# Three changes of order around the expert loop of a two-block transformer kernel: where the next stage's weight casts stand, where the router's transposes stand, and which engine sums the router's squares

## The chip, the cores and the metric

The kernel runs on one core of a Trainium2 chip, in one launch. The metric is the device time of that launch in microseconds (us); less is better. Times are medians over several runs, and one execution of each kernel is recorded by the hardware profiler.

## The reference

256 tokens of width 1024 in float32 pass through two transformer blocks. The stages at which the change works are the first block's mixture of experts and the feed-forward layer that follows it:

```python
def hierarchical_moe(h, ...):          # h = rmsnorm(x, norm_ffn_g)
    t = h.reshape(-1, D)
    p_group = softmax(t @ w_route_group + b_route_group)          # 4 groups, the best one is taken
    e_logits = t @ w_route_expert[g] + b_route_expert             # 8 experts in it, the best two are taken
    ...
    gates = ...                                                   # [32 experts, tokens]
    for wg, wu, wd, ge in experts:                                # 32 experts, width 512
        y = y + ge[:, None] * ((silu(t @ wg) * (t @ wu)) @ wd)
    return y
...
x = x + memory_cross_attention(...)                               # ends in @ w_mo
x = x + hierarchical_moe(rmsnorm(x, norm_ffn_g), ...)
x = rmsnorm(x, final_g)                                           # end of block 1
x = x + 0.5 * swiglu(rmsnorm(x, ffn1_norm), w13, w2)              # block 2 begins: the "first ffn"
```

Block 2 goes on with a linear recurrence, a second feed-forward layer, a shared key and value projection, a third feed-forward layer, stick-breaking attention of 16 heads and a fourth feed-forward layer.

## The kernel before, in words

The activations lie channels first, `xT` [128, 8 chunks, 256 tokens]. A normal product is three matmuls (lines 177 to 179): weights and activations are each split into a rounded part and a rest (`wh`, `wl` and `xgh`, `xgl`), and the product of the two rests is left out. `wload` (line 139) loads 1 MB of weights into a buffer `raw` by SyncE's queue (line 149), casts it to `wh` in two halves on ScalarE (ACT, line 157) and subtracts on VectorE (DVE, line 158).

The experts work in plain float32 on weights as loaded. 16 buffers form a ring for loads of 1 MB: 8 `raw`, 6 that `wh` and `wl` otherwise use, 2 that `xgh` and `xgl` otherwise use (`wraw`, line 161; DMA on line 171). An expert needs four loads `w_gu` and two `w_down`. A token takes a slot of 64 per expert.

- **Router** (`route`, line 696). Each block of two chunks of `xT` is finished on DVE (`update`, line 334) out of the last product's accumulators `acc0` to `acc3`. Its squares (ACT, line 272) are summed over channels by TensorE (PE) with one-column matmuls (line 275), 32 in all; `rstd` (line 291) and a chain of small DVE operations make the reciprocal root, copied to `my` (line 793). The logits are a product with 36 columns, copied to `lt` (line 716). `tokens` (line 805) transposes the normed input to tokens-first with 32 matmuls (line 813) and eight ACT copies (line 814); then the logits are transposed (line 721), scaled (`lg`, line 724), and some 25 DVE operations choose the experts (`ow`, `w`); line 743 counts positions on PE, one-hot matrices follow (line 831), then the gather by matmul (line 846) and the first expert product (line 941).
- **Expert loop** (`experts`, line 818). Per expert: `w_gu` products (line 941), `gu` on ACT (line 886), transposes (line 951), `sl` and `hx` (lines 953, 955), and one expert later the `w_down` products (line 967), `yh` on ACT (line 971), `yl` on DVE (line 972) and the scatter back to tokens by `combine` (line 982) into `acc0` to `acc3`. Expert 30 is followed by a branch (lines 799, 800), not taken here, for tokens beyond the 64 slots; the engines pass it together with SyncE.
- **First ffn** (`after_moe`, line 1022, then `ffn`). `update` adds the experts' sum to `xT`; squares on ACT and one-column sums on PE (again lines 272 and 275), splits (lines 221, 222), products.

A scheduler orders the instructions of each engine by their readiness in its own model, except where `after` (line 128) adds an order without a wait, as `pe` (line 925) does for the loop's matmuls while `s.queue` is a list. Matmul results go to two PSUM tags A and B of two buffers each, which `ps()` takes by turns unless a tag is named.

Of the kernel before, what the change touches and what calls it, by code (L numbers as in the profile page):

```python
# [8 lines left out]
F32 = mybir.dt.float32  # L9
# [3 lines left out]
ALU = mybir.AluOpType  # L13
# [3 lines left out]
P = 128  # L17
T = 256
D = 1024
KC = D // P  # L20
# [27 lines left out]
class Block:  # L48
    def __init__(s, ctx, tc, io):
        s.tc, s.nc, s.ctx, s.io = tc, tc.nc, ctx, io  # L50
        s.n = s.turn = s.place = 0
        s.queue = None
        pool = lambda name, bufs, **k: ctx.enter_context(tc.tile_pool(name=name, bufs=bufs, **k))
        s.cp = pool("const", 1)
        s.wp = pool("weights", 3)
        s.tp = pool("temps", 2)
        s.xp = pool("x", 1)
        s.pa = pool("acc", 1, space=PSUM)
        s.pp = pool("ps", 2, space=PSUM)
# [76 lines left out]
    def wload(s, views, C, N, parts=1, between=None):  # L136

        nc = s.nc
        full = C * N == 2048
        raw = s.new(s.wp, [P, 2048], "raw", F32, RAW)  # L140
        wh = s.new(s.wp, [P, 2048], "wh", F32R, WHL)
        wl = s.new(s.wp, [P, 2048], "wl", F32R, WHL)
        v = lambda t: t[:, :C * N].rearrange("p (c n) -> p c n", n=N)
        if not isinstance(views, list):
            n = C // parts
            views = [views[:, i * n:(i + 1) * n] for i in range(parts)]
        c = 0
        for i, view in enumerate(views):
            nc.sync.dma_start(v(raw)[:, c:c + view.shape[1]], view)
            c += view.shape[1]  # L150
            if between is not None:
                between(i)
        cuts = max(parts, 2) if full else parts
        n = C * N // cuts
        for i in range(cuts):
            lo, hi = i * n, (i + 1) * n
            nc.scalar.copy(wh[:, lo:hi], raw[:, lo:hi])  # L157
            nc.vector.tensor_sub(wl[:, lo:hi], raw[:, lo:hi], wh[:, lo:hi].bitcast(F32))  # L158
        return v(wh), v(wl)

    def wraw(s, view, C, N, n=None):
# [81 lines left out]
            nc.vector.scalar_tensor_tensor(y, u, 1.5, y, op0=ALU.add, op1=ALU.mult)  # L243
        return y

    def sums(s):

        return {"n": 0, "st": s.new(s.tp, [P, T], "ssq")}

    def ssq(s, st, x):  # L250

# [10 lines left out]
    def sums_pe(s, w=None):  # L262

        n = 1 if w is None else w.shape[2]
        return {"n": 0, "w": w, "pe": s.ps([P, 2, n], "B")}

    def ssq_pe(s, st, x, q=None):
        k, out = st["n"], st["pe"]
# [8 lines left out]
    def colsum(s, st, out):  # L277

        for h in range(2):
            s.nc.tensor.matmul(out[:, h:h + 1], st["st"][:, h * P:(h + 1) * P], s.ones[:, 0:1], start=True, stop=True)  # L280
        return out

    def bank(s, tag="acc3"):
# [45 lines left out]
    def update(s, ps, b, scale, xg, g, st):  # L329

        nc = s.nc
        xs = s.xT[:, 2 * b:2 * b + 2]
        if scale == 1.0:
            nc.vector.tensor_add(xs, ps, xs)
        else:
            nc.vector.scalar_tensor_tensor(xs, ps, scale, xs, op0=ALU.mult, op1=ALU.add)
        if xg is None:
            return
        if st is not None and "pe" in st:
            for m in (2 * b, 2 * b + 1):  # L340
                s.ssq_pe(st, s.xT[:, m])
        for m in (2 * b, 2 * b + 1):
            s.split(xg, m, s.xT[:, m], g[:, m:m + 1])
            if st is not None and "pe" not in st:
                s.ssq(st, s.xT[:, m])

    def rowproj(s, w, K):
# [30 lines left out]
                done(acc[b], b)  # L378
        return step, tail

    def residual(s, scale, g, sums=None):

        xg, st = s.pair(s.xp, KC, "xg"), (sums or s.sums)()
        return xg, st, lambda ps, b: s.update(ps, b, scale, xg, g, st)


# [239 lines left out]
    def mem_attention(s, p1, xg, rows, km, vm):  # L626
        nc, io = s.nc, s.io
# [39 lines left out]
        p = scores(0, query(0))  # L667
        for h in range(1, 4):
            q = query(h)
            pT = turn(p)  # L670
            p = scores(h, q)
# [2 lines left out]
        pT = turn(p)  # L674
        step(1, hl(1))
        values(3, pT)
        xg, st, done = s.residual(1.0, s.col("norm_ffn_g", 0, 8), s.sums_pe)
        tail([(2, hl(2)), (3, hl(3))], done)
        return xg, st

# [14 lines left out]
    def route(s, xg, rows):  # L695


        nc, t = s.nc, s.mt
# [5 lines left out]
        raw = s.tmp([P, P])  # L704
# [9 lines left out]
        s.proj(ps, wr, 0, xg, m=36)  # L714
        lt = s.new(t, [36, T], "lt")
        nc.vector.tensor_copy(lt, ps)
        s.tokens(xg)
        y = rows()
        pl = s.ps([P, 2, 36])
        for h in range(2):  # L720
            nc.tensor.transpose(pl[:, h], lt[:, h * P:(h + 1) * P], s.ident[0:36, 0:36])
        lg = s.new(t, [P, 2, 36], "lg")
        for h in range(2):
            nc.vector.scalar_tensor_tensor(lg[:, h], pl[:, h], y[:, h:h + 1], s.col("b_route", 0, 36), op0=ALU.mult, op1=ALU.add)
# [60 lines left out]
    def moe(s, mt, xg, st):  # L785
        nc = s.nc
        s.mt = mt
        y = []

        def rows():  # L790
            y.append(s.rstd(st["pe"].rearrange("p h n -> p (h n)"), D)[1])
            y.append(s.new(mt, [P, 2], "my"))
            nc.vector.tensor_copy(y[1], y[0])
            return y[0]
        pos, gs, gates, over, fi = s.route(xg, rows)
        with s.tc.tile_pool(name="experts", bufs=1) as me:
            def rest():

                flag = nc.values_load(fi[0:1, 0:1], min_val=0, max_val=1)
                with s.tc.If(flag > 0):  # L800
                    s.moe_over(over, y[1])
            acc = s.experts(me, pos, gs, gates, rest)
        return acc

    def tokens(s, xg):

        s.tok = s.pair(s.mt, 2, "tok", N=D)
        for k in range(0, KC, 2):
            for src, dst in zip(xg, s.tok):
                pt = s.ps([P, 2, 2, P])  # L810
                for j in range(2):
                    for h in range(2):
                        s.nc.tensor.matmul(pt[:, h, j], src[:, k + j, h * P:(h + 1) * P], s.idr, start=True, stop=True)
                s.nc.scalar.copy(dst[:, :, k * P:(k + 2) * P], pt.rearrange("p h j b -> p h (j b)"))

    def experts(s, mt, pos, gs, gates, rest):
# [141 lines left out]
    def expert_down(s, mt, e, hx, oT, gt):  # L958


        nc = s.nc
        pd = s.ps([P, 512], "A")
        for t in range(2):
            def use(w):
                for c in range(2):
                    for n in range(2):
                        s.pe(nc.tensor.matmul(pd[n * CAP:(n + 1) * CAP], hx[:, 2 * t + c], w[:, c, n * 512:n * 512 + 512],  # L967
                                              start=t + c == 0, stop=t + c == 2))
            s.expert_weights(use)
        yh, yl = (s.new(mt, [P, 512], n, F32R) for n in ("yh", "yl"))  # L970
        nc.scalar.mul(yh, pd, gt[:, 0:1])
        nc.vector.scalar_tensor_tensor(yl, pd, gt[:, 0:1], yh.bitcast(F32), op0=ALU.mult, op1=ALU.subtract)
        return yh, yl

    def combine(s, acc, e, y, oT):
# [325 lines left out]
    def run(s):  # L1301
# [8 lines left out]
        with tc.tile_pool(name="second", bufs=1) as p2:  # L1310
# [3 lines left out]
            ffn = lambda xg, rows, n, l, g, *more: s.ffn(  # L1314
                p2, xg, rows, io[f"ffn{n}_w13_2"][l], io[f"ffn{n}_w2_2"][l], g, *more)
            xg, rows = ffn(xg, rows, 1, 0, gains("mix_norm_2", 0), None, rescale)
            with tc.tile_pool(name="rglru", bufs=1) as pr:
                xg, rows = s.rglru(pr, xg, rows, gains("ffn2_norm_2", 0))
            with tc.tile_pool(name="attn", bufs=1) as pk:
# [82 lines left out]
```

## Time and profile before

| what | value |
|---|---|
| median of 3 runs | 1717.57 us (1716.57 to 1721.44) |
| the profiled execution's own time | 1718.19 us |
| its span in the profile | 1716.4 us, mean granted TensorE clock 0.984 |
| busy in the span | PE 97%, DVE 54%, ACT 41% |
| moved by DMA | 408 MB, 238 GB/s over the span |

The stages in the profiled span: mixer and memory attention to about 239 us, router to about 257, expert loop to about 705, last expert to about 731, first ffn from there on. PE's busy time is modelled in the profile, and the granted clock says at which share of its full speed TensorE ran. "Idle before" is an engine's waiting time ahead of an instruction, with what ended it.

### The profile page before, as it was taken

To read this page: it belongs to the slowest core of one execution; us is meant where nothing else is said; L and a number is where in the kernel's file an instruction comes from. 1 tells how busy PE (TensorE), PEld (TensorE's weight loads), DVE (VectorE), ACT (ScalarE), POOL (GpSimd) and SP (SyncE) were. 2 spreads that over 40 slices of the span, in tenths; PEclk is the share of its full clock that TensorE was granted. 3 is DMA by queue.
4 is the path that set the end of the run, shared out by engine and by line. 5 is a ranking of instruction groups with operands and counts; after the bars stand their busy time and mean duration, and the time that the engine had idled before them with its cause. 6 is when DMAs were issued, how large, how long until landed. Compare 5 with 4: busy or idle time off the path is not lost.

```text
span 1716.4 us, 28131 instructions
## 1 busy us (share of the span) xinstructions
PE 1659.7 (97%) x11883; PEld 1349.5 (79%) x11883; DVE 922.9 (54%) x1618; ACT 704.0 (41%) x1138; POOL 5.0 (0%) x19
## 2 busy tenths in 40 slices
PE   8999989999999998699999999999999999999998
PEld 7878984444444443299999999999899997689998
DVE  7998741111111110265657886556755558876554
ACT  8526532111111111244445754445644446764442
POOL 0000000000000000000000000000000000000000
PEclk9999989999999999889999999999999999899999
DMA  9334359999999999845553555554555454044530
GB/s 367 132 120 175 142 226 367 419 419 420 419 419 419 420 419 420 361 183 191 197 184 136 197 221 172 197 184 161 198 196 197 174 195 172 25 148 172 197 123 26
DMA packets 60227, 408.03 MB, mean 238 GB/s; under 512 B 6592, under 2 KB 9920, under 8 KB 11456
## 3 DMA queue, kind: packets, MB, share of 16 engines
q1 hardware_dynamic: 60096, 406.18, 61.4%
q8 instruction: 95, 1.56, 0.4%
q14 instruction: 36, 0.29, 0.0%
HBM read 405.11 MB, written 1.05 MB: 237 GB/s over the span
## 4 chain that ended last, share of the span: by engine, by line
PE 54%; DVE 2%; ACT 1%; issue 1%; DMA 0%; SPq 0%; ACTq 0%; DVEq 0%
PE A L179 6%; PE A L178 6%; PE A L177 6%; PE acc L177 5%; PE acc L178 5%; PE B L177 5%; PE B L178 5%; PE acc L179 5%; PE B L179 5%; ACT wh L157 1%; PE A L1262 1%; DVE wl L158 1%; PE A L967 1%; PE B L416 0%; PE B L408 0%
## 5 line engine op out<-in xcount | busy, mean ns | idle before, releaser
L157 ACT CAST wh<-raw 128x1024 fp32r<-128x1024 f32 (+2 forms) x378 | 378.0, 1034 | 445.0 <-issue 363.8
L158 DVE TENSOR_TENSOR wl<-raw,wh 128x1024 fp32r<-128x1024 f32 (+2 forms) x378 | 448.6, 1204 | 160.5 <-ACT wh L157 159.7
L177 PE MATMUL B<-xgh,wh 128*128 128x256 f32 x872 | 246.1, 282 | 6.9 <-ACT wh L157 6.9
L177 PE MATMUL A<-xgh,wh 128*128 128x256 f32 (+1 forms) x872 | 246.7, 283 | 0.0
L179 PE MATMUL A<-xgh,wl 128*128 128x256 f32 (+1 forms) x872 | 245.5, 282 | 0.1
L178 PE MATMUL A<-xgl,wh 128*128 128x256 f32 (+1 forms) x872 | 245.5, 282 | 0.1
L179 PE MATMUL B<-xgh,wl 128*128 128x256 f32 x872 | 245.6, 282 | 0.0
L178 PE MATMUL B<-xgl,wh 128*128 128x256 f32 x872 | 245.2, 281 | 0.0
L178 PE MATMUL acc<-hl,wh 128*128 128x256 f32 x704 | 194.7, 278 | 0.2
L179 PE MATMUL acc<-hh,wl 128*128 128x256 f32 x704 | 194.5, 277 | 0.0
L177 PE MATMUL acc<-hh,wh 128*128 128x256 f32 x704 | 193.1, 278 | 0.5 <-ACT hh L218 0.5
L177 PEld LDWEIGHTS B<-xgh,wh 128*128 128x128 f32 x872 | 164.5, 189 | 7.9 <-ACT wh L157 7.2
L179 PEld LDWEIGHTS B<-xgh,wl 128*128 128x128 f32 x872 | 164.4, 189 | 1.5 <-DVE wl L158 1.0
L178 PEld LDWEIGHTS A<-xgl,wh 128*128 128x128 f32 (+1 forms) x872 | 164.7, 189 | 0.6 <-DVE xgl L222 0.4
L177 PEld LDWEIGHTS A<-xgh,wh 128*128 128x128 f32 (+1 forms) x872 | 164.8, 189 | 0.3
L179 PEld LDWEIGHTS A<-xgh,wl 128*128 128x128 f32 (+1 forms) x872 | 164.7, 189 | 0.4 <-DVE wl L158 0.3
L178 PEld LDWEIGHTS B<-xgl,wh 128*128 128x128 f32 x872 | 164.7, 189 | 0.5 <-DVE xgl L222 0.2
L852 DVE COPY gx<-B 128x128 f32<-128x128 f32 x64 | 18.6, 291 | 231.9 <-PE B L846 223.6
L941 PE MATMUL A<-raw,gx 128*64 128x512 f32 x560 | 130.1, 603 | 8.6 <-DMA raw<-in_w_gu_dram 6.2
L178 PEld LDWEIGHTS acc<-hl,wh 128*128 128x128 f32 x704 | 132.1, 188 | 0.6 <-DVE hl L219 0.6
L179 PEld LDWEIGHTS acc<-hh,wl 128*128 128x128 f32 x704 | 132.2, 188 | 0.0
L177 PEld LDWEIGHTS acc<-hh,wh 128*128 128x128 f32 x704 | 130.9, 188 | 1.2 <-ACT hh L218 1.1
(407 smaller groups left out, 2422.4 us busy)
## 6 DMA issues: line engine op xcount, KB each, us to landing
raw<-in_ffn_w_dram SPq DMA_DIRECT2D x132, 1024.0 KB, 4.8
raw<-in_w_gu_dram SPq DMA_DIRECT2D x70, 1024.0 KB, 19.9
raw<-in_w_down_dram SPq DMA_DIRECT2D x34, 1024.0 KB, 19.9
wh<-in_w_gu_dram SPq DMA_DIRECT2D x22, 1024.0 KB, 19.9
wl<-in_w_gu_dram SPq DMA_DIRECT2D x22, 1024.0 KB, 19.9
wh<-in_w_down_dram SPq DMA_DIRECT2D x11, 1024.0 KB, 19.9
wl<-in_w_down_dram SPq DMA_DIRECT2D x11, 1024.0 KB, 19.9
raw<-in_a_w_in_dram SPq DMA_DIRECT2D x8, 1024.0 KB, 5.0
```

What stands on the lines that cost most here:

```text
L157: nc.scalar.copy(wh[:, lo:hi], raw[:, lo:hi])
L158: nc.vector.tensor_sub(wl[:, lo:hi], raw[:, lo:hi], wh[:, lo:hi].bitcast(F32))
L177: mm(out, w[0], x[0], start=first, stop=False)
L178: mm(out, w[0], x[1], start=False, stop=False)
L179: mm(out, w[1], x[0], start=False, stop=last)
L852: nc.vector.tensor_copy(dst, pg[:, :, i])
L941: s.pe(s.nc.tensor.matmul(ps[g * CAP:(g + 1) * CAP], gx[t // 2][:, 2 * (t % 2) + c], w[:, g, c * 512:c * 512 + 512], start=t + c == 0, sto ...
L967: s.pe(nc.tensor.matmul(pd[n * CAP:(n + 1) * CAP], hx[:, 2 * t + c], w[:, c, n * 512:n * 512 + 512], start=t + c == 0, stop=t + c == 2))
L1262: mm(sc[:, lo:lo + ke], qT[b:b + 64, c, qb * P:qb * P + P], kT[b:b + 64, c, 0:ke], start=True, stop=True)
```

## The change

The first part makes `expert_down` remember the instructions that write the last `yh` and `yl`; `wload` places its casts behind them, in program order on ACT and DVE, until the first ffn is built. The second part splits `tokens` in two: chunks 0 to 3, then the transposes of the logits (now in the bank of `acc0`), then chunks 4 to 7, in this order on PE. The third part takes the router's squares off PE: DVE adds them up (seven additions, the loop of `ssq`), and `colsum` sums over channels with two matmuls of one column, into the bank of `acc3`.

```diff
@@ class Block / wload @@
-        s.n = s.turn = s.place = 0
-        s.queue = None
+        s.n = s.turn = 0
+        s.queue = s.behind = None
...
-            nc.scalar.copy(wh[:, lo:hi], raw[:, lo:hi])
-            nc.vector.tensor_sub(wl[:, lo:hi], raw[:, lo:hi], wh[:, lo:hi].bitcast(F32))
+            act = nc.scalar.copy(wh[:, lo:hi], raw[:, lo:hi])
+            dve = nc.vector.tensor_sub(wl[:, lo:hi], raw[:, lo:hi], wh[:, lo:hi].bitcast(F32))
+            if s.behind is not None:
+                s.after(s.behind[0], act)
+                s.after(s.behind[1], dve)
@@ expert_down / run @@
-        nc.scalar.mul(yh, pd, gt[:, 0:1])
-        nc.vector.scalar_tensor_tensor(yl, pd, gt[:, 0:1], yh.bitcast(F32), op0=ALU.mult, op1=ALU.subtract)
+        s.behind = (nc.scalar.mul(yh, pd, gt[:, 0:1]),
+                    nc.vector.scalar_tensor_tensor(yl, pd, gt[:, 0:1], yh.bitcast(F32), op0=ALU.mult, op1=ALU.subtract))
...
             xg, rows = ffn(xg, rows, 1, 0, gains("mix_norm_2", 0), None, rescale)
+            s.behind = None
@@ route @@
-        s.tokens(xg)
+        s.queue = []
         y = rows()
-        pl = s.ps([P, 2, 36])
+        s.tokens(xg, (0, 2))
+        pl = s.pa.tile([P, 512], F32, name=s.nm("pl"), tag="acc0")[:, 0:72].rearrange("p (h n) -> p h n", h=2)
         for h in range(2):
-            nc.tensor.transpose(pl[:, h], lt[:, h * P:(h + 1) * P], s.ident[0:36, 0:36])
+            s.pe(nc.tensor.transpose(pl[:, h], lt[:, h * P:(h + 1) * P], s.ident[0:36, 0:36]))
+        s.tokens(xg, (4, 6))
+        s.queue = None
@@ mem_attention / moe / update @@
-        xg, st, done = s.residual(1.0, s.col("norm_ffn_g", 0, 8), s.sums_pe)
+        xg, st, done = s.residual(1.0, s.col("norm_ffn_g", 0, 8), True)
...
-            y.append(s.rstd(st["pe"].rearrange("p h n -> p (h n)"), D)[1])
+            y.append(s.rstd(s.colsum(st, s.bank()[1][:, 0:2]), D)[1])
...
-        if st is not None and "pe" in st:
-            for m in (2 * b, 2 * b + 1):
-                s.ssq_pe(st, s.xT[:, m])
-        for m in (2 * b, 2 * b + 1):
+        ms = (2 * b, 2 * b + 1)
+        if st is not None and st["first"]:
+            for m in ms:
+                (s.ssq_pe if "pe" in st else s.ssq)(st, s.xT[:, m])
+        for m in ms:
             s.split(xg, m, s.xT[:, m], g[:, m:m + 1])
-            if st is not None and "pe" not in st:
+            if st is not None and not st["first"]:
                 s.ssq(st, s.xT[:, m])
```

How the instructions stand on ScalarE just behind the branch after expert 30, before (`wh` is the first ffn's weights, `gu` and `sl` belong to expert 31, the two `yh` to experts 30 and 31, `sq` to the first ffn's norm):

```order
L800 UNCONDITIONAL_BRANCH
L157 CAST wh_6072<-raw_6071 128x1024
L886 ACTIVATE gu_5919<-A_5902,gt_5558 128x512
L157 CAST wh_6072<-raw_6071 128x1024
L953 ACTIVATE sl_5942<-A_5937 128x256
L157 CAST wh_6128<-raw_6127 128x1024 x2
L157 CAST wh_6231<-raw_6230 128x1024
L971 ACTIVATE yh_5955<-A_5946,gt_5480 128x512
L157 CAST wh_6231<-raw_6230 128x1024
L971 ACTIVATE yh_5968<-A_5959,gt_5558 128x512
L272 ACTIVATE sq_6018<-xT 128x256
```

The same place with the change:

```order
L807 UNCONDITIONAL_BRANCH
L894 ACTIVATE gu_5912<-A_5895,gt_5551 128x512
L961 ACTIVATE sl_5935<-A_5930 128x256
L979 ACTIVATE yh_5948<-A_5939,gt_5473 128x512
L979 ACTIVATE yh_5961<-A_5952,gt_5551 128x512
L157 CAST wh_6065<-raw_6064 128x1024 x2
L157 CAST wh_6121<-raw_6120 128x1024 x2
L275 ACTIVATE sq_6011<-xT 128x256
```

All six casts that stood ahead of `sq` were mixed with expert 31's work; now four stand there, all behind the last `yh`, and the third load's two casts have moved behind the squares.

On PE in the router, before (line 813 makes the tokens, line 721 transposes the logits, line 743 counts positions):

```order
L813 MATMUL A_2540<-idr_2497,xgl_2314 128x128 x4
L813 MATMUL B_2546<-idr_2497,xgh_2313 128x128 x4
L813 MATMUL A_2552<-idr_2497,xgl_2314 128x128 x4
L813 MATMUL B_2558<-idr_2497,xgh_2313 128x128 x4
L813 MATMUL A_2564<-idr_2497,xgl_2314 128x128 x4
L813 MATMUL B_2570<-idr_2497,xgh_2313 128x128 x4
L813 MATMUL A_2576<-idr_2497,xgl_2314 128x128 x4
L721 MATMUL B_2602<-ident,lt_2530 128x36 x2
L743 MATMUL A_2641<-ow_2637,up_2493 128x32
```

The same place with the change:

```order
L821 MATMUL A_2553<-idr_2487,xgl_2314 128x128 x4
L821 MATMUL B_2559<-idr_2487,xgh_2313 128x128 x4
L821 MATMUL A_2565<-idr_2487,xgl_2314 128x128 x4
L726 MATMUL pl_2571<-ident,lt_2520 128x36 x2
L821 MATMUL B_2574<-idr_2487,xgh_2313 128x128 x4
L821 MATMUL A_2580<-idr_2487,xgl_2314 128x128 x4
L821 MATMUL B_2586<-idr_2487,xgh_2313 128x128 x4
L821 MATMUL A_2592<-idr_2487,xgl_2314 128x128 x4
L750 MATMUL B_2634<-ow_2630,up_2483 128x32
```

The transposes have moved ahead of 16 token matmuls; the next `ps()` result after them, line 750's, has gone from tag A to tag B, since `pl` no longer takes a turn.

## Rows read from the trace of the kernel before

**Rows 1.** The page, part 2: PE's busy tenths in 40 slices of 42.9 us.
```profile
PE   8999989999999998699999999999999999999998
```

**Rows 2.** Windows: stretch, length, busy PE, PEld, DVE, ACT, POOL, granted clock, DMA share, GB/s.
```profile
246.00:248.50 2.50, 1.48 (x11) 1.20 (x10) 0.91 (x7) 2.50 (x6) 0.00 (x0) 1.00 1.02 433
248.50:258.70 10.20, 6.54 (x23) 5.07 (x23) 7.97 (x41) 1.80 (x8) 0.00 (x0) 0.50 1.01 420
258.70:265.00 6.30, 6.30 (x37) 3.58 (x38) 1.33 (x5) 1.43 (x5) 0.00 (x0) 1.00 0.40 117
...
270.00:700.00 430.00, 415.32 (x2385) 182.01 (x2385) 63.40 (x161) 75.49 (x179) 0.00 (x0) 1.00 1.01 419
...
709.50:723.00 13.50, 5.77 (x16) 2.20 (x18) 6.05 (x6) 5.88 (x7) 0.00 (x0) 0.50 0.84 333
...
733.60:746.60 13.00, 13.00 (x63) 13.00 (x62) 4.23 (x16) 4.25 (x11) 0.00 (x0) 0.50 0.50 206
```

**Rows 3.** Timeline of PE, router: start, duration, instruction, idle before it.
```profile
229.34 0.28 PE L178 MATMUL acc<-catl,wh 128*128 128x256 f32 x1
...
230.03 0.36 PE L179 MATMUL acc<-cath,wl 128*128 128x256 f32 x1
...
243.41 0.45 PE L813 MATMUL B<-idr,xgh 128*128 128x128 f32 x3
...
247.21 0.31 PE L721 MATMUL B<-ident,lt 36*128 36x36 f32 x2
251.57 0.37 PE L743 MATMUL A<-ow,up 128*128 128x32 f32 x1 [4.04 <-DVE w L763]
```

**Rows 4.** One line's instructions, lines 275 and 260: ns min/median/max, first and last start.
```profile
L275 PE MATMUL B<-ones,sq x32: 164/250/272, 229.6 to 241.7; 128*128 128x1 f32 x32
...
L260 DVE TENSOR_TENSOR ssq<-ssq,sq x13: 412/419/426, 109.7 to 175.1; 128x256 f32<-128x256 f32 x13
```

**Rows 5.** Timeline of DVE, router.
```profile
239.44 0.69 DVE L334 TENSOR_TENSOR xT<-acc,xT 128x512 f32<-128x512 f32 x1 [1.17 <-PE acc L179]
241.95 0.16 DVE L291 TENSOR_SCALAR nr<-B 128x2 f32<-128x2 f32 x1 [1.81 <-PE B L275]
...
245.35 0.17 DVE L793 COPY my<-nr 128x2 f32<-128x2 f32 x1
247.56 0.42 DVE L724 SCALAR_TENSOR_TENSOR lg<-B,nr,par 128x36 f32<-128x36 f32 x2 [2.04 <-PE B L721]
```

**Rows 6.** Timeline of SyncE's queue: the ring's first reissue.
```profile
263.77 5.48 SPq L171 DMA_DIRECT2D raw<-in_w_gu_dram  x4
```

**Rows 7.** Timeline of PE, end of the experts.
```profile
704.81 0.29 PE L982 MATMUL acc<-oT,yl 64*128 64x256 f32 x2
717.23 1.11 PE L951 MATMUL A<-ident,gu 128*128 128x128 f32 x4 [12.13 <-ACT gu L886]
718.28 9.39 PE L967 MATMUL A<-raw,hx 128*64 128x512 f32 x32
```

**Rows 8.** Timeline of ACT, end of the experts.
```profile
715.55 1.04 ACT L157 CAST wh<-raw 128x1024 fp32r<-128x1024 f32 x1 [22.09 <-DMA raw<-in_ffn_w_dram]
...
718.66 3.05 ACT L157 CAST wh<-raw 128x1024 fp32r<-128x1024 f32 x3
...
731.65 0.72 ACT L272 ACTIVATE sq<-xT 128x256 f32<-128x256 f32 x2 [2.22 <-DVE xT L334]
```

**Rows 9.** The chain that ended last, and line 800's events, at the branch.
```profile
710.60 4.92 DMA raw<-in_ffn_w_dram
...
L800 SPq EVENT_SEMAPHORE  x8: 17/17/17, 702.5 to 710.2; - x8
```

**Rows 10.** Timeline of PE late in the loop, full clock: one expert's `w_down`.
```profile
674.12 3.65 PE L967 MATMUL A<-raw,hx 128*64 128x512 f32 x16
```

**Rows 11.** Windows in the stick-breaking attention, columns as in rows 2.
```profile
1456.90:1470.75 13.85, 13.25 (x45) 8.33 (x46) 10.54 (x21) 9.75 (x21) 0.00 (x0) 0.51 0.00 1
...
1476.00:1515.00 39.00, 39.00 (x252) 30.21 (x250) 32.04 (x63) 29.14 (x63) 0.00 (x0) 1.00 0.14 47
```

More of the change, by code (lines that the diff above doesn't have):

```diff
@@ L244, in rsqrt, with sums @@
         return y
-    def sums(s):
-        return {"n": 0, "st": s.new(s.tp, [P, T], "ssq")}
+    def sums(s, first=False):
+        return {"n": 0, "first": first, "st": s.new(s.tp, [P, T], "ssq")}
     def ssq(s, st, x):
@@ L264, in sums_pe @@
         n = 1 if w is None else w.shape[2]
-        return {"n": 0, "w": w, "pe": s.ps([P, 2, n], "B")}
+        return {"n": 0, "first": True, "w": w, "pe": s.ps([P, 2, n], "B")}
     def ssq_pe(s, st, x, q=None):
@@ L279, in colsum @@
         for h in range(2):
-            s.nc.tensor.matmul(out[:, h:h + 1], st["st"][:, h * P:(h + 1) * P], s.ones[:, 0:1], start=True, stop=True)
+            s.pe(s.nc.tensor.matmul(out[:, h:h + 1], st["st"][:, h * P:(h + 1) * P], s.ones[:, 0:1], start=True, stop=True))
         return out
@@ L379, in rowproj, with residual @@
         return step, tail
-    def residual(s, scale, g, sums=None):
-        xg, st = s.pair(s.xp, KC, "xg"), (sums or s.sums)()
+    def residual(s, scale, g, first=False):
+        xg, st = s.pair(s.xp, KC, "xg"), s.sums(first)
         return xg, st, lambda ps, b: s.update(ps, b, scale, xg, g, st)
@@ L803, in moe, with tokens @@
         return acc
-    def tokens(s, xg):
-        s.tok = s.pair(s.mt, 2, "tok", N=D)
-        for k in range(0, KC, 2):
+    def tokens(s, xg, ks):
+        if 0 in ks:
+            s.tok = s.pair(s.mt, 2, "tok", N=D)
+        for k in ks:
             for src, dst in zip(xg, s.tok):
@@ L812, in tokens @@
                     for h in range(2):
-                        s.nc.tensor.matmul(pt[:, h, j], src[:, k + j, h * P:(h + 1) * P], s.idr, start=True, stop=True)
+                        s.pe(s.nc.tensor.matmul(pt[:, h, j], src[:, k + j, h * P:(h + 1) * P], s.idr, start=True, stop=True))
                 s.nc.scalar.copy(dst[:, :, k * P:(k + 2) * P], pt.rearrange("p h j b -> p h (j b)"))
```

## The prediction

> **What bounds the kernel now.** I read the page's slices first: PE is busy nearly everywhere; the slice from 686 to 729 us has a 6, the one from 215 to 257 an 8 [rows 1]. So only a stretch in which PE waits, or runs at the lower of its two clock levels, can give time back. The windows show two such places near the change: the router, 248.5 to 258.7 us, at granted clock 0.50 (1.2 GHz), and the end of the experts, 709.5 to 723 us, where PE is busy for 5.8 of 13.5 us at 0.50 [rows 2]. Between them the loop moves 419 GB/s with the DMA engines full [rows 2]. So the loop's end is set by its loads, and a router that ends earlier helps only if the loads follow it. They do: the ring's first slots are asked for again at 263.77, when the first expert products have read them [rows 6], and the loop runs on from that point.
>
> The timelines then say what ends last. In the router, PE waits 4.04 us for DVE ahead of line 743 [rows 3], and DVE had waited 2.04 us for the logits' transposes [rows 5], which stand behind all tokens. At the end of the experts PE waits 12.13 us for ScalarE's `gu` [rows 7]; the row ahead of `gu` on ScalarE is a cast that waited for the first ffn's weights [rows 8], whose load was issued only at 710.60 and took 4.92 us [rows 9].
>
> **Part three and part two, the router.** The 32 one-column matmuls go [rows 4]. What they cost is read from the gaps between products: 229.34 to 230.03 is 0.69 us where two products normally follow each other in 0.12 (a product's 0.28 is its pipelined length), so 0.57 for a group of four; with its neighbours and the second, shorter group about 1.1 us for a block's eight [rows 3]. Three blocks' sums stand ahead of the last `xT`, which so comes 3.3 us earlier, 236.1 instead of 239.44 [rows 5]. In their place DVE gets seven additions of 0.42 us, 2.9 in all [rows 4]; two per block lie in DVE's waits for the accumulators (1.17 us ahead of the last `xT` [rows 5]), and only the last stands on the path. From the last `xT`: 0.69 for itself, 0.72 for two squares (the ScalarE form of [rows 8]), 0.42 for the addition, two matmuls of 0.25 with handovers 0.7: the column sums are there at 238.7, against 241.95 [rows 5]. From there to `my` it takes 3.6 us with two splits and `lt` in between [rows 5]; I take 3.4, so `y` is ready at 242.1.
>
> The logits' product ends 4.4 us earlier (four times 1.1) than the tokens' row at 243.41, at 239.0. All tokens took from 243.41 to 247.21, so half takes 2.0 [rows 3], and the transposes stand at 241.0 to 241.4. `lg` needs both: 242.1, against 247.56, **5.5 us earlier**. The other 16 token matmuls, 2 us, now run while DVE chooses experts (3.6 us from `lg` to line 743's operand); if that cover were gone they would cost 2. PSUM buffers `acc0` and `acc3` are free by then, since their `xT` has been written.
>
> The ends: the small operations could be held up by the additions and splits on DVE, worth 1.5 us, gain 4.0. Or the clock could stay high: PE then idles about 2 us less, and of the 6.5 us that it was busy at the lower level [rows 2] half, 3.3, would be saved at most; 2.5 of it counts, since the first matmuls of that stretch stand inside DVE's chain: gain 8.0. I take 5.5, because the pattern stays: PE was busy for 1.48 of the 2.5 us ahead of the fall [rows 2], and it will again have waits there. The ring's loads start up to 3.5 us earlier too, because the buffers they fill are read out earlier, so they don't take over as the bound.
>
> **Part one, the end of the experts.** All times in this paragraph are those of before; the router's gain shifts them. The combine of expert 29 ends at 705.10 [rows 7]. `gu` of expert 31 needs products that PE finished ahead of that combine, so it is no longer late, and the transposes start at 705.1 instead of 717.23; they take at most 1.1 [rows 7], expert 30's `w_down` then 3.65 at full clock [rows 10], to 709.9. Expert 31's needs its last load. SyncE's wait at the branch lasts until 710.2, when the loop's last load has landed [rows 9], so the product ends at about 713.5, and I allow 3 us for `yh`, `yl` and the combine (nothing is queued ahead of them): `xT` at about 717, some 14 us ahead of the square's row, which follows it at once [rows 8]. The added order holds nothing else up: the casts can't start before 715.5 anyway, because SyncE issues their loads at 710.60 as before [rows 9].
>
> Not all of it stays. The squares stand behind four casts. Two need the first load (715.55), two the second. The second lands between 718.0 (2.5 us per MB at 419 GB/s [rows 2]) and 718.66, when a cast of it ran without a wait [rows 8]. Two casts of 1.04 us later it is 720.1 to 720.7: the first square at 720.4 instead of 731.65 [rows 8], **11.3 us earlier**, and some 3 us of the gain is given to the load's landing. Behind that PE has the same work, 13.0 us of it at the lower level from 733.6 [rows 2]. PE again waits (about 4 us) ahead of this work, so I keep that stretch. The third load's casts are now behind the squares; two loads give PE 96 products (8 chunks, 2 blocks, 3 parts each), 11 us even at the 0.12 of full clock, which covers them. The ends: 9.0, if expert 30's and 31's products run at the lower level as now (9.39 against 7.3 us, [rows 7, 10]); 14.3, if the casts held nothing; the clock is a rival, below.
>
> On the load there is a rule to weigh. Its row says 4.92 us for 1 MB from issue to landing. The Trainium skill's page "DMA: Bandwidth & Descriptors", in "Anatomy of one DMA", gives about 2.0 us fixed plus the bytes at 436 GB/s, an estimate of 4.4 us here, and says it of transfers that GpSimd issues; by it the squares would start 0.5 us earlier and the sum be 1700.9. The trace's duration is used.
>
> **Side effect.** With `pl` out of the turns, tags A and B swap for everything behind, and in the stick-breaking attention, which mixes turned and named tags, PE's and DVE's order around the first heads changes. Elsewhere PE is full and buffers are symmetric. A low-clock stretch with 13.25 us of PE's work lies there [rows 11]. If it vanished, at most half of that, 6.6 us, would be gained; if it came half as long again, as much lost. I take zero, in the middle, because the work and most of its order stay.
>
> **The sum.** 5.5 + 11.3 = 16.8 us off the profiled execution's 1718.2 (span 1716.4): **1701.4**. That execution lies 0.6 above the median, so I say 1701. A measurement of this kernel can tell about 0.3%, 5.2 us, from no change.
>
> **Rivals.**
> 1. *The clock stays high as well* in the router (2.5 us more) or behind the experts, where 13.0 us at the lower level would be 6.5: 1701 less 2.5 to 9.0, 1692 to 1698.5, middle 1695.5. For it: PE's long wait of 12.13 us shrinks to about 4. Against: in both places waits remain. 0.17.
> 2. *The loop takes the router's gain back*, because its loads, not its start, set its end: only 11.3 is left, 1706.9. For it: 419 GB/s throughout. Against: from 258.7 to 265 the DMA engines are at 0.40 [rows 2], because the ring waits for its readers. 0.12.
> 3. *The end's gain is lost to the casts*, if the loads land later under the loop's last ones, or the first ffn then waits for the third load's casts: only the router's 5.5, 1712.7. 0.05.
> 4. *Slower, by the swapped tags.* In the attention the clock is low for 13.85 us after waits of PE, and then high through 39.0 us of full work [rows 11]. If the new order made PE wait there again and the low level lasted through these 39 us, they would take up to 39 us longer, 1740. It decides from 16.8 us, some 17 us of full-clock work done at half the level. Against: the reordering touches the first four heads only. 0.03.
> 5. *The change doesn't do what it says*: the orders are without waits, so the casts might still take ScalarE first; 1718. The listed order speaks against it. 0.02.
>
> **How the numbers follow.** Forecast 0.61, 1701, its own range 1697 to 1706; rivals as above, 0.39. Faster by over 0.3% (below 1712.4): forecast, 1, 2 and half of 3, 0.92. Within 0.3%: half of 3, most of 5, 0.05. Slower: 0.03. The range takes in most of rival 1 and rival 2, 1693 to 1708.
>
> **What would show it.** Right: line 275's rows gone from the router; the logits scaled 4 to 7 us earlier and SyncE's first reissue at about 258; PE's 12 us wait gone and `gu` the first ScalarE row behind the branch; the first ffn's squares directly behind a fourth cast and not behind `xT`. Wrong: a reissue at 262 or later, line 291 later than 240, the loop's end not following the reissue, squares behind something other than a cast, a low-clock stretch that has moved or vanished, or a longer low-clock stretch in the attention.

## The result and the profile after

The changed kernel takes 1705.4 us (median of 4 runs, 1703.37 to 1707.55), the kernel before 1717.76 (4 runs): a ratio of 0.992, 95% interval 0.990 to 0.994. That is 12.4 us less, 10 to 17 by the interval. The forecast was 1701, 16.8 us less, in a range of 1693 to 1708. The profiled execution took 1703.37 us (span 1701.6, granted clock 0.984), 14.8 us less than that of before.

The page's second part, PE's slices and the clock's (42.5 us each):

```profile
PE   8999999999999998899999999999999998999998
...
PEclk9999999999999999899999999999999999799999
```

The dips of [rows 1] at the router and at the experts' end are a 9 and an 8 now; the lowest clock is now a 7, in the slice from 1446 us, in the attention.

The timeline of PE and then of DVE in the router, which answer to [rows 3] and [rows 5]:

```profile
238.58 0.58 PE L283 MATMUL st<-ones,ssq 128*128 128x1 f32 x4
...
241.42 0.31 PE L726 MATMUL pl<-ident,lt 36*128 36x36 f32 x2
...
246.04 0.36 PE L750 MATMUL B<-ow,up 128*128 128x32 f32 x1 [2.17 <-DVE w L769]
```

```profile
236.25 0.68 DVE L337 TENSOR_TENSOR xT<-acc,xT 128x512 f32<-128x512 f32 x1
...
239.19 0.16 DVE L294 TENSOR_SCALAR nr<-st 128x2 f32<-128x2 f32 x1
...
241.94 0.17 DVE L800 COPY my<-nr 128x2 f32<-128x2 f32 x1
242.02 0.41 DVE L731 SCALAR_TENSOR_TENSOR lg<-pl,nr,par 128x36 f32<-128x36 f32 x2
```

`lg` waits for nothing any more: root and transposes are ready within 0.4 us of each other. It starts at 242.02, 5.5 us ahead of before. SyncE's queue follows: the first reissue, 263.77 in [rows 6], and then the first ffn's loads, 710.60 in [rows 9], are both 5.9 to 6.0 us earlier.

```profile
257.78 5.48 SPq L174 DMA_DIRECT2D raw<-in_w_gu_dram  x4
...
704.73 23.03 SPq L149 DMA_DIRECT2D raw<-in_ffn_w_dram  x11
```

At the experts' end, PE and ACT, for [rows 7] and [rows 8]:

```profile
691.22 9.27 PE L949 MATMUL A<-raw,gx 128*64 128x512 f32 x32 [4.55 <-PEq L807]
...
701.57 0.66 PE L959 MATMUL A<-ident,gu 128*128 128x128 f32 x4
702.16 7.09 PE L975 MATMUL A<-raw,hx 128*64 128x512 f32 x32
...
715.14 1.05 PE L278 MATMUL B<-nr,sq 128*128 128x2 f32 x8 [2.21 <-ACT sq L275]
```

```profile
710.31 0.69 ACT L979 ACTIVATE yh<-A,gt 128x512 fp32r<-128x512 f32 x1 [3.77 <-PE acc L990]
710.90 3.87 ACT L157 CAST wh<-raw 128x1024 fp32r<-128x1024 f32 x4
714.67 0.72 ACT L275 ACTIVATE sq<-xT 128x256 f32<-128x256 f32 x2
```

The wait of 12.13 us ahead of the transposes is gone, `w_down` runs at full clock, and the first square stands directly behind the fourth cast, at 714.67 instead of 731.65: 16.98 us earlier, of which 5.9 come from the router. From there on the two kernels keep their distance up to the attention. The windows show where it then changes; columns as in [rows 2]:

```profile
245.20:251.70 6.50, 5.06 (x20) 4.66 (x21) 5.33 (x21) 1.39 (x5) 0.00 (x0) 0.50 1.00 417
716.40:729.60 13.20, 13.20 (x63) 13.11 (x63) 9.05 (x20) 6.36 (x14) 0.00 (x0) 0.50 1.01 419
1439.90:1463.30 23.40, 20.30 (x67) 12.95 (x68) 15.93 (x32) 13.81 (x29) 0.00 (x0) 0.50 0.12 46
```

The low-clock stretch in the router is shorter (6.5 us for 10.2), the one behind the experts as long as before (13.2 for 13.0), and the one in the attention is 23.4 us long instead of 13.85 [rows 11]. The first of these does not go with the change: in the experiments below, two kernels with before's sums (behind_only, transposes_only) have the short stretch in the router, and two with the new sums (squares_only, squares_ordered) the long one.

Stage by stage, from the starts of the rows that bound them (us; `ssq` stands for the matmuls that sum squares over channels, which also open and close the attention). The labels are those of the experiments below.

| stage | before | changed | after_again | turn_kept | behind_only | early_squares |
|---|---|---|---|---|---|---|
| start to the `ssq` at 177 | 177.31 | 177.18 | 180.17 | 178.61 | 177.98 | 177.53 |
| to the scaled logits | 70.25 | 64.84 | 64.90 | 64.87 | 70.34 | 64.89 |
| to the ring's first reissue | 16.21 | 15.76 | 15.90 | 16.15 | 15.23 | 15.90 |
| to the first ffn's load | 446.83 | 446.95 | 447.04 | 446.29 | 446.70 | 447.27 |
| to its first square | 21.05 | 9.94 | 10.19 | 10.83 | 9.14 | 8.21 |
| to the first ffn's closing `ssq` | 201.99 | 201.93 | 203.73 | 204.55 | 202.59 | 199.39 |
| three more stages | 506.20 | 506.11 | 506.53 | 506.19 | 506.70 | 505.99 |
| attention | 96.50 | 100.41 | 94.43 | 97.04 | 96.86 | 95.88 |
| last ffn, to PE's last matmul | 175.31 | 173.71 | 174.25 | 173.71 | 175.30 | 175.30 |

Router and experts' end give 5.4 + 0.45 + 11.1 = 17.0 us in the changed kernel. In its first trace the attention takes 3.9 back and the last ffn gives 1.6. The 0.45 is no more than scatter: in the experiments this stage takes 15.2 to 16.5 us where TensorE's waits in the router aren't filled, and 15.23 in behind_only, whose router is before's.

In the attention, with the tags swapped, PE waits longer for VectorE ahead of the transposes of the second half's queries. Before, changed and turn_only (below):

```profile
1457.50 0.47 PE L1210 MATMUL B<-ident,qk 128*128 128x128 f32 x1 [1.46 <-DVE qk L1201]
```

```profile
1440.32 0.45 PE L1218 MATMUL A<-ident,qk 128*128 128x128 f32 x1 [3.62 <-DVE qk L1209]
```

```profile
1461.69 0.44 PE L1211 MATMUL A<-ident,qk 128*128 128x128 f32 x1 [3.62 <-DVE qk L1202]
```

### The profile page after: what moved, and what is told of

Its sections match the earlier page's. It is cut to its first block, busy times and chain, and to the rows that moved or that the text cites. A ratio compares the mean times of both kernels' runs of the same rounds, so it can differ in the third digit from the quotient of the medians.

```text
span 1701.6 us, 28091 instructions
## 1 busy us (share of the span) xinstructions
PE 1654.1 (97%) x11855; PEld 1345.1 (79%) x11855; DVE 924.5 (54%) x1625; ACT 704.3 (41%) x1138; POOL 5.0 (0%) x19
## 4 chain that ended last, share of the span: by engine, by line
PE 53%; DVE 2%; ACT 2%; issue 1%; ACTq 0%
PE A L180 6%; PE A L181 6%; PE A L182 6%; PE acc L180 5%; PE acc L181 5%; PE B L180 5%; PE B L181 5%; PE B L182 5%; PE acc L182 5%; ACT wh L157 1%; PE A L1270 1%; DVE wl L158 1%; PE B L420 1%; PE B L188 0%; PE A L188 0%
```

## The experiments

The first question: theory T says that the two gains hold, and that the swapped tags A and B cost 4 us in the attention; its rival, that the 4 us are chance of single executions. Further kernels take the parts alone, place the casts otherwise and fill TensorE's waits. They ran in three groups of four, 4 to 12 executions each, with the kernel before beside each group. Its median was 1720.84, 1720.07 and 1721.13 us there (1717.76 beside the result), so gains below are worked out from the ratio to before, with 1717.76 for before.

**after_again.** The changed kernel, unedited.

> The changed kernel once more, beside the others. Theory T: the router and the experts' end give 17 us, as in its first trace (first square of the first ffn 16.98 us earlier), and the swapped tags A and B give some 4 us back in the stick-breaking attention, where TensorE waits longer for VectorE and its low-clock stretch lasts 23.5 us instead of 13.9; the time is 1703 to 1706. Rival: the 4 us are chance of single executions; then the profiled attention is as long as before's in some executions and the time scatters down to 1700.5.

1706.06 us, ratio 0.993 (0.991 to 0.995). Its profiled attention took 94.43 us, 2 us less than before's, with a low-clock stretch that lies between 1446 and 1454:

```profile
1428.46:1446.00 17.54, 13.60 (x69) 10.74 (x67) 16.33 (x57) 11.72 (x19) 0.00 (x0) 1.00 0.59 215
1446.00:1454.00 8.00, 5.60 (x23) 3.69 (x23) 6.22 (x12) 5.70 (x10) 0.00 (x0) 0.57 0.00 1
```

So the same program spends 23 us of its attention at the lower level in one execution and about 7 in another, 6 us apart in time. PE's wait of 3.62 us ahead of the query transposes is there in both. Two other executions, at a mean granted clock of 0.980, took 1711.41 and 1713.73; the one at 0.989 took 1703.77. The program's start scatters too: this execution reached the `ssq` at 180.17, 3 us late, ahead of everything that the change touches.

**turn_kept.** The change with the tags of before.

```diff
         s.tokens(xg, (4, 6))
         s.queue = None
+        s.turn = 1 - s.turn
```

> The change, with the turn of tags A and B moved on by one where the logits' transposes used to take it, so that everything behind the router has the tags of before. T: the attention takes its order of before, its low-clock stretch is about 14 us again, and the time is some 4 us below the changed kernel's: 1700.5, with the first square of the first ffn at 714.7 as in the changed kernel. Rival (the 4 us are chance): the same time as the changed kernel, 1703 to 1706.

1704.69 us, ratio 0.990 (0.989 to 0.992), so 16.7 us below before, the forecast's gain. PE's wait ahead of the query transposes is 1.46 us again, as before. Its low stretch there was 17 us, though, and its median is only 1.4 us below after_again's; the intervals overlap.

**turn_only.** Before with the tags swapped.

```diff
         pl = s.ps([P, 2, 36])
+        s.turn = 1 - s.turn
```

> The kernel before, with the tags swapped behind the router and nothing else changed. T: 4 us slower than before, 1721.5, all of it in the attention, with a low-clock stretch of 20 us or more there. Rival (chance): as before, 1717 to 1718.

1722.14 us, ratio 1.0005 (0.999 to 1.002): no difference. But the times fall apart: three executions with a mean clock of 0.985 to 0.987 took 1714.98 to 1717.86, the nine others, at 0.977 to 0.982, took 1720.18 to 1728.63. The profiled one is of the long kind, with PE's wait of 3.62 us and an attention of 100.3 us:

```profile
1460.00:1485.00 25.00, 20.62 (x68) 13.21 (x69) 17.38 (x36) 15.27 (x32) 0.00 (x0) 0.52 0.16 57
```

**swapped_early.** Run in the third group: the kernel early_squares (below) without the line that keeps the tags.

> The kernel with the later casts (early squares), but with the tags A and B swapped behind the router, as in the change. Theory T (swapped tags cost some 4 us on average, because in most executions the low-clock stretch of the attention gets longer): 0.25 percentage points above the early squares' ratio of 0.9883, so 0.991, 1703 to 1704, with a wide scatter (attention 94 to 100.5 us). Rival (what is left between the change and the change with its tags kept is chance): 0.988 to 0.989, 1699 to 1700.

1700.59 us, ratio 0.988 (0.986 to 0.990), while early_squares has 0.988 (0.987 to 0.990) in its group. The profiled attention took 100.0 us, again with 24 us at the lower level. In all traces together the attention was long in three of four executions of the swapped order (100.4, 94.4, 100.3, 100.0), while the order of before gave 95.9 to 97.8 in seven. PE's wait ahead of the query transposes goes with the order without exception: 3.62 us in these four, 1.46 in these seven (before, turn_kept, behind_only, the three router kernels and early_squares). The time shows no clear cost: by the ratios the three comparisons give 4.5, 0.9 and minus 1.0 us, with 2.6 to 4.2 us to either side; weighted by these widths, 1.2 with 1.9 to either side. T's cost of 4 us isn't borne out as a mean, and a smaller one isn't excluded; a longer wait of PE and a wider scatter are what the swapped order shows.

**behind_only.** Part one alone, in the kernel before: the diffs of `wload`, `expert_down` and `run` that stand ahead, and nothing else.

> The kernel before with part one alone: the first ffn's casts behind the last expert's results on ScalarE and VectorE; router and tags as before. T: the first square of the first ffn comes 11 us earlier, at 720.5 instead of 731.65, and nothing is given back: 1706.5. Rival: the gain at the experts' end needs the router's earlier loads as well (they change when the last loads land); then less than 9 us, 1709 or more.

1709.47 us, ratio 0.994 (0.993 to 0.995): 10.7 us less. Here the casts do wait for the loads, as the prediction had it. ACT, after the loads' issue at 710.25:

```profile
715.00 1.99 ACT L157 CAST wh<-raw 128x1024 fp32r<-128x1024 f32 x2 [1.74 <-DMA raw<-in_ffn_w_dram]
717.49 1.99 ACT L157 CAST wh<-raw 128x1024 fp32r<-128x1024 f32 x2 [0.50 <-DMA raw<-in_ffn_w_dram]
719.39 0.72 ACT L275 ACTIVATE sq<-xT 128x256 f32<-128x256 f32 x2
```

The square is 12.3 us earlier, 11.9 counted from the load's issue. The load took at most 4.75 us to its cast, close to [rows 9]. The estimate of 4.4 by the Trainium skill's page "DMA: Bandwidth & Descriptors", "Anatomy of one DMA", lies below both.

**transposes_only, squares_only, squares_ordered.** The router's parts, each with casts and tags of before. The first takes `residual` and `rows` back to the sums on PE:

```diff
-        xg, st, done = s.residual(1.0, s.col("norm_ffn_g", 0, 8), True)
+        xg, st, done = s.residual(1.0, s.col("norm_ffn_g", 0, 8), s.sums_pe)
...
-            y.append(s.rstd(s.colsum(st, s.bank()[1][:, 0:2]), D)[1])
+            y.append(s.rstd(st["pe"].rearrange("p h n -> p (h n)"), D)[1])
```

> Part two alone: the logits' transposes ahead of half of the tokens'; squares summed on TensorE and casts as before; tags as before. Theory T: the logits then wait for the root, which is ready where it was (245.5), so they are scaled 2.0 us earlier; the first reissue of the ring and the end of the loop follow, 1716 where before is 1718. Counted from the column sums at 177 us, which lie ahead of every change, to the scaled logits: 68.2 us, where before has 70.25 and the full change 64.9. Rival: the transposes were what ended last, and moving them gives most of the 5.4 us: 66 us or less.

1717.91 us, ratio 0.9985 (0.997 to 0.9995); 68.39 us to the scaled logits, 1.9 less than before, close to T's 2.0. The root, not the transposes, now ends last. The second puts all tokens first again:

```diff
-        s.queue = []
+        s.tokens(xg, (0, 2, 4, 6))
         y = rows()
-        s.tokens(xg, (0, 2))
-        pl = s.pa.tile([P, 512], F32, name=s.nm("pl"), tag="acc0")[:, 0:72].rearrange("p (h n) -> p h n", h=2)
+        pl = s.ps([P, 2, 36])
...
-        s.tokens(xg, (4, 6))
-        s.queue = None
```

> Part three alone: squares summed on VectorE, the logits' transposes behind all tokens, casts as before, tags as before. T: the 32 one-column matmuls leave TensorE, so tokens and transposes end 4.4 us earlier and the logits with them: 65.9 us from the column sums at 177 us to the scaled logits (before 70.25), 1713.5 where before is 1718. Rival: VectorE's additions hold the root up, so that less than 3 us are left, 67.3 us or more.

1718.25 us, ratio 0.999 (0.998 to 0.9999); 68.79 us to the logits, 1.5 less, where I expected 4.4. PE and then DVE show that it was neither VectorE's additions nor the tokens, but a place in PE's order:

```profile
242.67 0.61 PE L818 MATMUL A<-idr,xgl 128*128 128x128 f32 x4
243.11 0.56 PE L283 MATMUL st<-ones,ssq 128*128 128x1 f32 x4
243.59 0.31 PE L725 MATMUL B<-ident,lt 36*128 36x36 f32 x2
```

```profile
243.70 0.16 DVE L294 TENSOR_SCALAR nr<-st 128x2 f32<-128x2 f32 x1 [3.27 <-PE st L283]
```

The column sums stand behind all tokens, and the root starts 3.3 us after VectorE was free. So the third kernel writes the order out:

```diff
-        s.tokens(xg, (0, 2, 4, 6))
+        s.queue = []
         y = rows()
+        s.tokens(xg, (0, 2, 4, 6))
...
-            nc.tensor.transpose(pl[:, h], lt[:, h * P:(h + 1) * P], s.ident[0:36, 0:36])
+            s.pe(nc.tensor.transpose(pl[:, h], lt[:, h * P:(h + 1) * P], s.ident[0:36, 0:36]))
+        s.queue = None
```

> Part three alone once more (squares summed on VectorE, transposes behind all tokens, casts and tags as before), but with TensorE's order written out, so that the two column-sum matmuls stand ahead of the tokens; alone and unordered they had been placed behind all of them, at 243.11. Theory T: that place was why part three alone gave only 1.5 us; now the logits are scaled 65.9 to 66.3 us from the column sums at 177 us (68.8 unordered, 64.9 in the full change) and the time is 4 us below before's, ratio 0.9975. Rival: VectorE's chain was late by itself; 67.5 us or more.

1716.2 us, ratio 0.997 (0.996 to 0.998), 4.6 us less; 67.03 us to the logits, 3.2 less, between the two expectations. The order was worth 1.8 of the unordered kernel's 68.79. The root is ready at 242.6 and the transposes end last again:

```profile
244.78 0.42 DVE L730 SCALAR_TENSOR_TENSOR lg<-B,nr,par 128x36 f32<-128x36 f32 x2 [2.04 <-PE B L726]
```

**early_squares.** The change with its tags kept, and the casts placed otherwise: on ACT only the first load's two casts ahead of the squares, the later loads' behind the second block's split (as built: behind all squares); on DVE the subtractions behind the first `xT`. `made` and `added` are the last split's and the last update's instructions.

```diff
+        if s.behind is not None and s.stages:
+            s.behind = s.stages.pop(0)
         return v(wh), v(wl)
...
             s.update(acc[b], b, 1.0, xg, gg, st)
+            if b == 0:
+                s.behind = (s.behind[0], s.added)
+            if b == 1:
+                s.stages = [s.made]
```

> The change with the tags of before, and with the casts placed otherwise: only the first load's two casts stand ahead of the first ffn's squares on ScalarE, the second load's behind the squares and splits of the second block, and on VectorE the additions to xT stand ahead of the first load's subtractions. T: the first square follows xT at once and comes 0.9 us earlier, at some 10 us from SyncE's leaving the branch to the square instead of 10.4 to 11.2; the time is 0 to 1 us below that of the change with the tags kept. Rival: TensorE then runs dry, because the second load's weights come later; 1 us or more above it.

1699.59 us, ratio 0.988 (0.987 to 0.990): 20.1 us below before, and clear of the changed kernel's first interval (0.990 to 0.994). Below turn_kept, whose tags it shares, it lies by 3.4 us where 0 to 1 was expected, though these two intervals overlap. The first square comes 8.21 us after the load's issue instead of 9.9 to 10.8, and the stage behind it is 2.6 us shorter than before's as well, with a low-clock stretch of half the length. The three other kernels with these casts (swapped_early, filled_right, filled_all) repeat it: 8.0 to 8.7 us to the square, and a stretch of 6.8 to 10.2 us, from the clock's fall to its rise, where the ten other traces have 13.6 to 17.1. PE's wait ahead of the sums is 0.76 us where the change has 2.21:

```profile
714.27 1.05 PE L280 MATMUL B<-nr,sq 128*128 128x2 f32 x8 [0.76 <-ACT sq L277]
```

```profile
717.50:724.30 6.80, 6.80 (x34) 6.80 (x35) 6.68 (x10) 6.06 (x10) 0.00 (x0) 0.52 1.02 423
```

**filled_heads, filled_right, filled_all.** Does the clock stay up in the attention where TensorE's waits are filled? Unread matmuls in a free bank, in TensorE's order where it waits; `weights` and `queries` put their first matmul behind the last of them:

```diff
-        zs[0] = weights(0)
-        zs[1] = weights(1)
-        queries(1)
+        zs[0] = weights(0, s.fill(9, last, pb))
+        zs[1] = weights(1, s.fill(6, s.scored, pb))
+        queries(1, s.fill(12, s.scored, pb))
```

> The change with the tags of before, and 27 matmuls whose results nobody reads (9, 6 and 12, of ones with a chunk of xT, into a free bank) placed where TensorE waits at the start of the attention: ahead of the first scores, of the second, and of the second half's query transposes. Theory C: what spreads the times of one and the same kernel is the clock, which falls when TensorE waits there; with the waits filled the granted clock stays at 1.00 through the attention, its time from the first column sums of the attention (line 280's last but one) to the last ones falls from 96.8 us to some 90, and the total is 5 to 7 us below that of the change with the tags kept, with less scatter. Rival: the waits don't decide; the low stretch is there all the same, and the time is the same or longer by up to 1 us.

1706.92 us, ratio 0.992 (0.991 to 0.994), above turn_kept's 0.990 where 5 to 7 us below it was expected, though the clock stays up through the whole stage, as the window says. The timeline behind it shows why: the nine fillers ahead of the first scores take 4.05 us, where turn_kept's wait is 0.97. They stand as 18 records, since a matmul of plain float32 leaves two here (54 for the 27 fillers; the rounded form of the next kernel leaves 27).

```profile
1426.00:1526.50 100.50, 96.94 (x596) 77.42 (x594) 79.76 (x175) 66.91 (x132) 0.00 (x0) 1.00 0.25 92
```

```profile
1438.64 4.05 PE L289 MATMUL st<-xT,ones 128*128 128x256 f32 x18
1442.62 0.92 PE L1281 MATMUL A<-kT,qT 64*128 64x128 f32 x4
```

filled_right is early_squares with the same three places filled by the rounded form (`s.fill(9, last, pb, xg[0][:, 1, 0:P], xg[0][:, 0])` and so on):

> Early squares, and in the attention's three waits the 9, 6 and 12 unread matmuls again, now of the rounded float32 form with 256 columns (0.12 us each, 3.2 in all, where the plain float32 ones took some 0.44 each and 12 in all, three to four times the waits they were to fill). Theory C: the granted clock stays at 1.00 in the attention and this time nothing is delayed; the stage from the column sums ahead of it to those behind it falls from 96 to 90 us, the total to 1693 to 1694, ratio 0.985. Rival: VectorE and ScalarE set the pace of the first heads, so that a faster TensorE only waits more; stage 94 us or more, ratio 0.988.

1699.49 us, ratio 0.988 (0.986 to 0.990), no faster than early_squares. The profiled attention took 92.68 us at granted clock 1.00, 3.2 less than early_squares' 95.88, where 6 were expected; 1.7 us went into waits of PE for VectorE's and ScalarE's results that early_squares doesn't have (0.42, 0.64 and 0.26 new, 1.06 for 0.71). filled_all adds the router:

```diff
         s.tokens(xg, (4, 6))
+        s.fill(20, s.queue[0], s.bank("acc1")[0][:, 0:P], s.idr, s.idr)
         s.queue = None
```

> The same, and 20 more unread matmuls (128 columns, 0.11 us each, 2.2 in all) behind the last tokens in the router, where TensorE waits 2.2 us for VectorE. Theory C: no fall of the clock in the router; the first reissue of the ring comes 13.2 us behind the scaled logits instead of 15.9, and the total is 2.7 us below the kernel without them, 1691, ratio 0.9835. Rival: the waits that follow among the counting matmuls let the clock fall all the same; then nothing changes, or the low stretch comes later and lies on more work, 1 us longer.

1698.32 us, ratio 0.987 (0.985 to 0.989), the lowest of all, but its interval overlaps those of early_squares and filled_right. Below filled_right it lies by 1.2 us by the medians and 2.7, the gain expected, by the ratios, with some 4.5 to either side: not shown. The router's clock no longer falls, and the reissue comes 13.94 us after the logits instead of 15.90; all other traces have 15.2 to 16.5. The windows of filled_all and of early_squares:

```profile
243.00:258.00 15.00, 14.16 (x93) 10.38 (x94) 10.28 (x53) 6.19 (x19) 0.00 (x0) 1.00 0.99 413
```

```profile
243.00:258.00 15.00, 12.33 (x61) 9.13 (x62) 9.81 (x49) 5.61 (x18) 0.00 (x0) 0.77 0.94 393
```

In this profiled execution the clock fell in the attention nevertheless, between 1445 and 1453, with the same fillers that had kept it up in filled_right's.

## Why the prediction was right, point by point, and where its numbers were off

- **The router, 5.5 us.** Measured 5.4 from a mark ahead of the change. The last `xT` came at 236.25 (236.1 said), `my` at 241.94 (242.1), the transposes at 241.42 (241.0). Line 294 came 0.5 us later than said, since it stands behind two splits on VectorE, and its chain was as much shorter, for the same reason. squares_ordered and transposes_only show the two waits that end here: the new sums alone give 3.2 us, the new place of the transposes alone 1.9, both 5.4. One term was too large: the logits' product ends 3.5 us earlier, not 4.4, counted from the mark at 177 us (its last row before, then changed), since the column sums, a wait of 0.17 us and token matmuls stand among its rows. It cost nothing, because the root came last of all (241.91, the transposes 241.73). The "32 one-column matmuls" are 32 records of 16 matmuls (line 283's four records are two); what they cost was read from times, so the sum stands.

```profile
243.29 0.28 PE L179 MATMUL A<-xgh,wl 128*36 128x256 f32 x1
```

```profile
239.70 0.28 PE L182 MATMUL A<-xgh,wl 128*36 128x256 f32 x1
```

- **The loop follows.** From reissue to the first ffn's load 446.83 us before and 446.3 to 448.1 in all the others: rival 2 is out. Its 1706.9 lies nearer to the measured 1705.4 than the forecast does; only the traces tell the two apart.
- **The experts' end, 11.3 us.** Measured 11.1 in the changed kernel, 10.7 in the total of behind_only. The size was right and a step behind it was not: "the first square at 720.4", set by the second load's landing, holds for behind_only (719.39, with waits for both loads). In the full change the step "The added order holds nothing else up" failed: by the 4.92 us of [rows 9] the first load had landed at about 709.65, an estimate, and the first cast began only at 710.90, behind `yh` of expert 31, which came late, at 710.31. The buffer of `yh` is single, so it waits for the combine of expert 30 (3.77 us), and PE had waited 2.1 us longer at the branch than before (4.55 for 2.44 us). The two chains differ by little, so the sum came out the same; to that extent its size is luck.
- **The clock behind the experts.** 13.2 us at the lower level, as kept in the sum; rival 1 did not occur in the changed kernel. Half of it did in early_squares, where PE's wait is 0.76 us and the stretch half as long.
- **The side effect.** "I take zero" is the step by which the forecast's 16.8 us and the 14.8 of the profiled execution differ: the attention took 3.9 us more there, within the bounds of 6.6, with a low-clock stretch of 23.4 us. It is rival 4's mechanism in a small form, and the one sign of being wrong that the prediction listed and that came ("a longer low-clock stretch in the attention"); its four signs of being right came as well. That the swapped tags make PE wait longer there is shown, 3.62 us for 1.46 in turn_only too, where only they differ. That they cost time on average is not: three comparisons give no clear cost, and one execution of the same program was 2 us shorter than before's.
- **The sum.** 17.0 us at the first ffn's square, where 16.8 were forecast. What is left between 16.8 and the medians' 12.4 is what lies outside the change, and scatters: the start by 3 us, the attention by 6, the first ffn by 2.6 (201.9 to 204.6 us in the columns with the change's casts, with a low-clock stretch of 13.6 to 17.1 us). turn_kept measured 16.7. Which of these holds the median of the changed kernel 2 us above its profiled execution stays open, since the other executions left no trace to read.

## What to carry to other kernels

An instruction that waits for a transfer belongs behind everything on its in-order engine that doesn't need it: one cast ahead of `gu` cost 11 us here, and which of the remaining chains then ends last (the load in one kernel, a single result buffer in another) is read again after the move. Where two chains end at the same operation, moving one gives only what the other allows: part two alone gave 1.9 us, then the root ended last. And a part is worth what its built order lets it be: part three gave 1.5 us with its column sums behind all tokens and 3.2 with them ahead; both parts together 5.4. After a change ask also what a counter shared with the rest of the program, such as a turn of buffers, does to the order of stages that weren't meant, and measure with a mark ahead of the change, because a start that scatters by 3 us hides a gain of 5.

## What the runs showed that was not expected

The low-clock stretch in the attention isn't a property of the program alone: about 7 or about 24 us in two executions of the same kernel, the same code and inputs. Unread matmuls in TensorE's waits went with a granted clock of 1.00 in two of the three attentions that had them, but the stage became 3.2 us shorter at best rather than 6, and the medians show nothing of it.

TensorE's own branch instruction behind expert 30 has two lengths, and they go with the program: 3.09 to 3.21 us in before, turn_only, behind_only and transposes_only, 5.95 to 6.23 in all ten traces of kernels whose router sums its squares on VectorE.

```profile
L800 PEldq COMPARE_BRANCH  x1: 3090/3090/3090, 690.8 to 690.8; - x1
```

```profile
L807 PEldq COMPARE_BRANCH  x1: 6049/6049/6049, 684.8 to 684.8; - x1
```

The first is before's, the second the changed kernel's. The 3 us are mostly hidden by the loads: from the reissue to the first ffn's load it takes 446.3 to 448.1 us with either length. behind_only, with the short one, reaches the square 0.8 us sooner after its load than the change does (9.14 against 9.94). No kernel varied it, but the traces show what the branch ends on: a packet of queue q8, which part 3 of the profile's page calls "instruction". In each of the 14 traces one of 16 KB takes 1.07 to 1.08 us during the branch, and the branch ends 1.41 to 1.43 us behind it. In the short branch it starts 0.6 to 0.7 us after the branch, in the long one 3.5 to 3.7. Why it starts later there stays open.
